# Modulation rows made by GpSimd inside the attention, in paced pieces, with loads from its own queue

## The chip, the core and the metric

One core of a Trainium2 chip runs the whole layer in one launch. The engines are TensorE (PE), VectorE (DVE), ScalarE (ACT), GpSimd (POOL) and SyncE (SP), each with its own instruction stream that it runs in order; they meet by semaphores. The metric is the device time in microseconds (us).

## The reference, cut to what matters

One layer of a diffusion backbone: 1024 latent tokens and 256 context tokens, width 1024, fp32. The part that the change touches:

```python
mod = jnp.einsum('bd,de->be', jax.nn.silu(c), w_mod[layer]) + b_mod[layer]
sh1, sc1, g1, sh2, sc2, g2 = jnp.split(mod[:, None, :], N_MOD, axis=-1)
hx = modulate(rmsnorm(x, norm1_g[layer]), sh1, sc1)          # h * (1 + scale) + shift
q_x, k_x, v_x, u_x, b_x, c_x, ga_x, gc_x = split_projection(hx @ w_in[layer])
o_attn = latent_window_attention(q, k, v, k_ctx, v_ctx, attn_sink[layer])
y_conv = short_conv_mixer(u_x, b_x, c_x, conv_w[layer])      # B * conv3(C * u)
x = x + g1 * gated_merge(o_attn, y_conv, ga_x, gc_x, w_proj_attn, w_proj_conv, w_out)
hx2 = modulate(rmsnorm(x, norm2_g[layer]), sh2, sc2)
x = x + g2 * expert_choice_moe(hx2, ...)
```

The modulation rows g1, sh2, sc2 and g2 (parts 2 to 5 of mod, 1024 values each) are each a product of one vector, silu(c), with a 1024x1024 piece of w_mod. They are first read behind the products stage below.

## The kernel before

The program runs five stages, one behind the other: the modulation for the first norm, the norm and the projections of q, k and v (to 252 us); the attention (252 to 582); the products stage (611 to 1085); output projection, second norm and router; the experts (from 1234). Products in fp32 are made from a high and a low part of each operand: three matmuls each.

**Attention.** A unit is one of 4 key groups and one of 8 blocks of 128 queries: 32 units, numbered n. In the loop over units (L690 on) the step s of unit n first transposes the softmax rows p of one block of keys (`turn`, L630; ACT L633 and DVE L634 split the result), then makes the scores of one head of unit n+2 (`scores`, L605/606; DVE L608; exponential on ACT L613); behind the fourth head GpSimd scales that unit's four p tiles (`normalise`, L625). Then `pour(1)` takes one step of the gate projection (three matmuls, L40/42/44), a filler for TensorE, and `values` makes two matmuls (L642/643). The order of the engines' instructions is set by the scheduler from this code, each engine's stream being fixed when the program is built. At units 4, 10, 16 and 22 `x_sums` is emitted: ten additions or subtractions of 128x512 on GpSimd (L657), splits on ACT and DVE, and writes.

**Products stage.** 20 pairs of column blocks, each multiplied by Strassen's scheme in Winograd's form: seven block products (slots 0 to 6) of 12 matmuls of 128x512 (L795), 84 per pair. Here the order of all engines is written out by hand (`in_order`); `at_turn(n, slot, f)` puts work at a slot of pair n. VectorE makes each pair's weight sums (L829/830, L839/840), splits (L810) and results (L1107, L1140, `quad` L867 to L889; L875 is the addition q<-q or q<-psT,q). Pairs 2, 5, 8 and 11 add the convolution: ACT L907, then four steps on VectorE (L908, L910), both operands in SBUF. Beside it:

- `Row` (four rows): each load of 128x1024 from w_mod goes out on SP's queue (L740), ScalarE scales it by silu(c) (L743), GpSimd adds it to the sum (L745); then a split (ACT L751, POOL L752), and `total` at slot 6 of pairs 2, 5, 8 and 12: four matmuls with a column of ones (L760), two additions of the bias on VectorE (L761), a write to rowd (L766).
- `sums_of` on GpSimd (L930): four subtractions of 128x512 for each block of the convolution's output (pairs 4, 7, 10, 13) and four for each of four blocks of the attention's output (`o_rows`, turns 17, 38, 59 and 68, in pairs 2, 5, 8 and 9).
- From pair 11 on, the operands of the next products are split by ACT (L973) and VectorE and GpSimd (L974), and two multiplications move to GpSimd (L881, L980).

Of the kernel before, what the change touches and what calls it, by code (L numbers as in the profile page):

```python
# [27 lines left out]
def hybrid_layer(ctx, tc, x, c, cx, c_ctx, w_mod, b_mod, norm1_g, w_in, attn_sink, conv_w,  # L28
# [702 lines left out]

    class Row:


        def __init__(self, n, part):
            self.n, self.part, self.w = n, part, {}

        def load(self, k):
            self.w[k] = mp_slot(4 + k % 2 if k else 6)
            nc.sync.dma_start(out=self.w[k], in_=w_mod[k * 128:(k + 1) * 128, self.part * 1024:self.part * 1024 + 1024])  # L740

        def add(self, k):
            nc.scalar.activation(out=self.w[k], in_=self.w[k], func=AF.Copy, scale=sf[:, 0, k:k + 1])  # L743
            if k:
                nc.gpsimd.tensor_tensor(out=self.acc, in0=self.w[k], in1=self.acc, op=OP.add)  # L745
            else:
                self.acc = self.w[k]

        def split(self):
            self.halves = [mp.tile([128, 1024], FR, name=f"mp{4 + i}") for i in range(2)]  # L750
            nc.scalar.copy(out=self.halves[0], in_=self.acc)  # L751
            nc.gpsimd.tensor_tensor(out=self.halves[1], in0=self.acc, in1=self.halves[0].bitcast(F32), op=OP.subtract)  # L752
            self.row = self.acc[0:1]
            nc.gpsimd.dma_start(out=self.row, in_=b_mod[:, self.part * 1024:self.part * 1024 + 1024])

        def total(self, pf):
            br = self.row
            for hf in range(2):
                for i in range(2):
                    nc.tensor.matmul(pf[hf][0:1], lhsT=onesr, rhs=self.halves[i][:, hf * 512:hf * 512 + 512], start=(i == 0), stop=(i == 1))  # L760
# [1093 lines left out]
```

## Time and profile before

| what | us |
|---|---|
| median of 3 runs (1834.47 to 1837.97) | 1836.47 |
| the profiled run | 1830.33 |
| its span | 1828.5 |
| busy in the span: PE / DVE / ACT / POOL | 1716.5 / 1459.1 / 1040.5 / 557.4 |
| attention, 330.0 us: PE / POOL busy | 327.0 / 138.8 |
| pairs 0 to 10, 261.6 us (611 to 872.6): PE / DVE / POOL busy | 228.1 / 206.1 / 129.1 |
| output projection to router, 148.7 us: PE busy | 121.4 |
| experts, 594.0 us: PE / DVE busy, DMA share | 580.8 / 559.7, 0.93 |

The table is read by stage: a span has one engine that limits it in one stage and another in the next. Durations are those of one profiled execution, so a sum is made against 1830.33 and then set beside the median. The granted clock of TensorE is a share of its higher level, 2.4 GHz; 0.50 is the lower level, 1.2 GHz.

### The profile page before, as it was taken

What the parts mean: (1) busy time and instruction counts of PE and PEld (TensorE: products, weight loads), DVE (VectorE), ACT (ScalarE), POOL (GpSimd) and SP (SyncE); (2) the same over time, 40 slices, a digit from 0 to 9 for tenths busy, and PEclk for the clock granted to TensorE, in tenths of its full rate; (3) what the DMA queues carried; (4) which work ended last, traced back from release to release, by engine and by line L of the source; (5) the groups of instructions that cost most, each with busy time, mean ns of one, the idle gap of its engine ahead of it and who ended that gap; (6) DMA issues with size and microseconds to landing.
All of it is one profiled execution on the core that took longest, in us unless ns stands there. A gap on an engine that the chain in (4) does not pass through costs nothing.

```text
span 1828.5 us, 24343 instructions
## 1 busy us (share of the span) xinstructions
PE 1716.5 (94%) x8421; PEld 1384.8 (76%) x8421; DVE 1459.1 (80%) x1996; ACT 1040.5 (57%) x1482; POOL 557.4 (30%) x366
## 2 busy tenths in 40 slices
PE   8999999999999989878798898959999999999997
PEld 5778888888888867666567677847888888888875
DVE  6756568778775488897887876578999999999997
ACT  6642267767774334333445343226777877877875
POOL 0001226255231245365763301241024223223101
PEclk8999999999999999998899999979999999999999
DMA  9353354344413737437657245778999999999955
GB/s 343 129 162 115 127 189 142 94 138 126 148 55 121 255 107 220 133 121 230 230 160 252 72 151 190 257 280 323 341 398 396 387 393 399 384 397 398 340 196 196
DMA packets 210861, 415.71 MB, mean 227 GB/s; under 512 B 17643, under 2 KB 107051, under 8 KB 209202
## 3 DMA queue, kind: packets, MB, share of 16 engines
q1 hardware_dynamic: 182226, 368.20, 56.3%
q0 software_dynamic: 6912, 25.51, 4.7%
q10 hardware_dynamic: 21600, 20.45, 3.2%
q8 instruction: 66, 1.08, 0.2%
q14 instruction: 57, 0.47, 0.1%
HBM read 343.31 MB, written 70.80 MB: 226 GB/s over the span
## 4 chain that ended last, share of the span: by engine, by line
PE 63%; DVE 14%; issue 4%; ACT 2%; DMA 2%; POOL 1%; SPq 0%; ACTq 0%; POOLq 0%; DVEq 0%
PE psA L1659 19%; PE psB L1659 5%; PE psF L1659 5%; PE w L795 5%; PE psT L630 3%; PE psT L795 3%; PE psA L1225 3%; PE psF L40 2%; PE psF L42 2%; PE psF L44 2%; PE psB L643 2%; PE psB L642 2%; PE psA L605 2%; PE psA L606 2%; DVE x L810 2%
## 5 line engine op out<-in xcount | busy, mean ns | idle before, releaser
L1659 PE MATMUL psA<-part,xeh 128*128 128x512 f32 x1024 | 281.9, 392 | 0.5 <-ACT xeh L1647 0.5
L1659 PEld LDWEIGHTS psA<-part,xeh 128*128 128x128 f32 x1024 | 191.3, 188 | 39.9 <-ACT xeh L1647 1.0
L1694 POOL DMA_INDIRECT md<-ye,idxs x15 | 107.9, 7190 | 213.3 <-DVE ye L1691 213.3
L1659 PE MATMUL psA<-part,xel 128*128 128x512 f32 x512 | 163.4, 390 | 0.0
L625 POOL TENSOR_SCALAR p<-p,l 128x640 f32<-128x640 f32 (+1 forms) x128 | 99.6, 797 | 176.5 <-DVE l L623 51.3
L1517 DVE TENSOR_TENSOR part<-er,part 128x1024 fp32r<-128x1024 f32 x118 | 138.4, 1219 | 5.3 <-ACT part L1515 2.0
L1515 ACT CAST part<-er 128x1024 fp32r<-128x1024 f32 x118 | 123.7, 1056 | 32.9 <-PE psA L1659 19.9
L809 ACT CAST whi<-raw 128x1024 fp32r<-128x1024 f32 x40 | 42.0, 1049 | 173.7 <-DVE raw L840 110.0
L634 DVE TENSOR_TENSOR tl<-psT,th 128x512 fp32r<-128x512 f32 x152 | 103.9, 687 | 26.5 <-ACT th L633 25.1
L608 DVE CUSTOM_DVE_ANT_0 sn<-psA,msk,nsink 128x640 f32<-128x640 f32 (+1 forms) x128 | 107.3, 843 | 21.7 <-PE psA L606 21.1
L745 POOL TENSOR_TENSOR mp<-mp,mp 128x1024 f32<-128x1024 f32 x28 | 73.3, 2618 | 152.5 <-ACT mp L743 151.7
L633 ACT CAST th<-psT 128x512 fp32r<-128x512 f32 x152 | 88.3, 584 | 50.4 <-PE psT L630 49.5
L613 ACT ACTIVATE p<-sn,nm 128x640 f32<-128x640 f32 (+1 forms) x128 | 103.0, 806 | 19.5 <-DVE nm L608 17.6
L1659 PEld LDWEIGHTS psA<-part,xel 128*128 128x128 f32 x512 | 96.3, 188 | 20.5 <-DVE xel L1648 0.3
L1517 DVE TENSOR_TENSOR part<-mh,part 128x1024 fp32r<-128x1024 f32 x88 | 105.0, 1219 | 5.4 <-ACT part L1515 2.4
L1517 DVE TENSOR_TENSOR part<-ml,part 128x1024 fp32r<-128x1024 f32 x88 | 105.3, 1219 | 4.4 <-ACT part L1515 1.6
L1515 ACT CAST part<-ml 128x1024 fp32r<-128x1024 f32 x88 | 92.2, 1052 | 26.3 <-PE psA L1659 17.6
L1515 ACT CAST part<-mh 128x1024 fp32r<-128x1024 f32 x88 | 92.1, 1052 | 25.2 <-PE psA L1659 16.5
L1517 DVE TENSOR_TENSOR part<-mp,part 128x1024 fp32r<-128x1024 f32 x85 | 100.8, 1220 | 6.6 <-ACT part L1515 3.8
L1515 ACT CAST part<-mp 128x1024 fp32r<-128x1024 f32 x88 | 91.9, 1052 | 24.5 <-PE psA L1659 16.1
L1659 PE MATMUL psB<-part,hhh 128*128 128x512 f32 x256 | 98.6, 396 | 0.2 <-ACT hhh L1647 0.2
L810 DVE TENSOR_TENSOR wlo<-raw,whi 128x1024 fp32r<-128x1024 f32 x40 | 52.9, 1322 | 55.4 <-ACT whi L809 55.4
(501 smaller groups left out, 4695.4 us busy)
## 6 DMA issues: line engine op xcount, KB each, us to landing
raw<-in_w_in_dram SPq DMA_DIRECT2D x49, 512.0 KB, 5.2
er<-in_w_exp_down_dram SPq DMA_DIRECT2D x47, 512.0 KB, 8.7
er<-in_w_exp_up_dram SPq DMA_DIRECT2D x38, 512.0 KB, 6.0
mp<-in_w_exp_gate_dram SPq DMA_DIRECT2D x36, 512.0 KB, 6.3
mh<-in_w_exp_up_dram SPq DMA_DIRECT2D x33, 512.0 KB, 5.6
ml<-in_w_exp_up_dram SPq DMA_DIRECT2D x33, 512.0 KB, 6.5
mp<-in_w_mod_dram SPq DMA_DIRECT2D x32, 512.0 KB, 4.9
er<-in_w_exp_gate_dram SPq DMA_DIRECT2D x32, 512.0 KB, 5.8
```

The costliest lines, as they stand in the source:

```text
L608: nc.vector.tensor_tensor_reduce(out=sn, in0=sp[:, 512 - n:768], in1=msk.rearrange("p a b -> p (a b)")[:, mo * 128:mo * 128 + n + L], op0= ...
L613: nc.scalar.activation(out=p, in_=sn, func=AF.Exp, scale=-1.0, bias=self.nm4[:, h:h + 1], accum_out=self.l4[:, h:h + 1])
L625: nc.gpsimd.tensor_scalar(self.pr[h], self.pr[h], l4[:, h:h + 1], 1.0, op0=OP.mult, op1=OP.mult)
L633: nc.scalar.copy(out=th, in_=pt)
L634: nc.vector.tensor_tensor(out=tl, in0=pt, in1=th.bitcast(F32), op=OP.subtract)
L745: nc.gpsimd.tensor_tensor(out=self.acc, in0=self.w[k], in1=self.acc, op=OP.add)
L795: nc.tensor.matmul(ps_, lhsT=w[a][:, o + k], rhs=xs[b][:, k], start=(first and k + a + b == 0), stop=(k == 3 and a == 1), skip_group_check ...
L810: tt(out=lo, in0=src, in1=hi.bitcast(F32), op=OP.subtract)
L1515: nc.scalar.copy(out=hi, in_=raw)
L1517: eng.tensor_tensor(out=lo, in0=raw, in1=hi.bitcast(F32), op=OP.subtract)
L1659: nc.tensor.matmul(outs[s], lhsT=lh[:, k], rhs=wt[:, s * 512:s * 512 + 512], start=(k == 0 and n == 0), stop=(k == NK - 1 and n == 2))
L1694: nc.gpsimd.indirect_dma_start(out=md, out_offset=bass.IndirectOffsetOnAxis(ap=idxs[:, e:e + 1], axis=0), in_=ye, in_offset=None, compute_ ...
```

## The change

The class `Row` goes. A generator, `mod_row(n)`, makes a row on GpSimd alone: it loads 128x1024 of w_mod from GpSimd's own queue, scales it (L716), adds it to the sum (L718), issues the next load, and hands back; then bias loads; then two matmuls with columns of `onehot` (L730) put the two halves of the sum of all partitions on two rows, VectorE adds the bias (L731), and SP writes rowd. The loaded tile "o2" has one buffer, and so has the sum "o1". `x_sums` hands back three times in between, and `o_sums` makes the subtractions for two of the attention's four blocks. `pool_work` chains four rows, four x_sums and two o_sums; the attention's loop takes one piece at s = 1 and one at s = 4 of every unit, so a row is 10 pieces, five units. In the products stage the subtractions for the convolution's output and for the two other blocks go to VectorE, and the two quads of the last pair move behind the first matmuls of the output projection and the router's row.

```diff
+    onehot = consts.tile([128, 4], F32, name="onehot")
...
+        for i in range(3):
+            nc.vector.tensor_scalar(onehot[:, i:i + 1], ones, float(i == 1), None, op0=OP.mult)
...
+    os_cm = tc.tile_pool(name="os", bufs=1)
+    osp = os_cm.__enter__()
+
+    def mod_row(n):
+        part = n + 2
+        acc = osp.tile([128, 1024], F32, name="o1")
+
+        def load(k):
+            w = osp.tile([128, 1024], F32, name="o2")
+            nc.gpsimd.dma_start(out=w, in_=w_mod[k * 128:(k + 1) * 128, part * 1024:part * 1024 + 1024])
+            return w
+
+        w = load(0)
+        yield
+        for k in range(NK):
+            nc.gpsimd.tensor_scalar(w if k else acc, w, sf[:, 0, k:k + 1], 1.0, op0=OP.mult, op1=OP.mult)
+            if k:
+                nc.gpsimd.tensor_tensor(out=acc, in0=w, in1=acc, op=OP.add)
+            if k < NK - 1:
+                w = load(k + 1)
+                yield
+        small = osp.tile([128, 1024], F32, name="o2")
+        br, nr = small[0:2, 0:512], small[0:2, 512:1024]
+        nc.gpsimd.dma_start(out=br, in_=b_mod[:, part * 1024:part * 1024 + 1024].rearrange("o (h f) -> (o h) f", h=2))
+        if part == 4:
+            nc.gpsimd.dma_start(out=nr, in_=norm2_g.rearrange("o (h f) -> (o h) f", h=2))
+        yield
+        pf = psT()[0:2]
+        for hf in range(2):
+            nc.tensor.matmul(pf, lhsT=onehot[:, 1 - hf:3 - hf], rhs=acc[:, hf * 512:hf * 512 + 512], start=(hf == 0), stop=(hf == 1))
+        nc.vector.tensor_tensor(out=br, in0=pf, in1=br, op=OP.add)
+        if part == 4:
+            nc.vector.scalar_tensor_tensor(out=br, in0=br, scalar=1.0, in1=nr, op0=OP.add, op1=OP.mult)
+        nc.sync.dma_start(out=rowd[n].rearrange("(h f) -> h f", h=2), in_=br)
+        yield
+
+    def pool_work():
+        for n in range(4):
+            yield from mod_row(n)
+        for ks in range(4):
+            yield from x_sums(ks)
+        for ks in range(2):
+            yield from o_sums(ks)
+
+    def o_sums(ks):
+        o1, o2 = (osp.tile([128, 2, 512], F32, name=f"o{a}") for a in (1, 2))
+        o = o_rows(ks, o1.rearrange("p a b -> p (a b)"), [o2[:, 0], o2[:, 1]])
+        yield
+        sums_of(nc.gpsimd, *o)
+        sums_out(*o)
+        yield
+
+    pool_left = pool_work()
...
-        if n in (4, 10, 16, 22):
-            x_sums((n - 4) // 6)
...
             pour(1)
+            if s in (1, 4):
+                next(pool_left, None)
             if s > 0:
                 cur.values(s - 1)
+    for _ in pool_left:
+        pass
     at_cm.__exit__(None, None, None)
+    os_cm.__exit__(None, None, None)
...
-    class Row:
...
     for m in range(4):
-        at_turn(3 * m + 4, 2, lambda: sums_of(*st["ys"]))
+        at_turn(3 * m + 4, 2, lambda: sums_of(nc.vector, *st["ys"]))
         at_turn(3 * m + 4, 5, lambda: sums_out(*st["ys"]))
 
-    def row_start(r):
-        st["row"] = Row(r, r + 2)
-
-    for r in range(4):
-        at_turn(3 * r, 0, lambda r=r: row_start(r))
-        for k, (a, b) in enumerate(((0, 2), (1, 3), (2, 4), (5, 7), (6, 8), (9, 11), (10, 12), (13, 15))):
-            at_turn(3 * r, a, lambda k=k: st["row"].load(k))
-            at_turn(3 * r, b, lambda k=k: st["row"].add(k))
-        at_turn(*((3 * r + 2, 2) if r < 3 else (11, 6)), lambda: st["row"].split())
-
-    for ks, b in enumerate((17, 38, 59, 68)):
-        at_turn(0, b - 5, lambda ks=ks: o_rows(ks))
-        at_turn(0, b, lambda: sums_of(*st["o"]))
+    for ks, b in ((2, 17), (3, 38)):
+        at_turn(0, b - 5, lambda ks=ks: o_late(ks))
+        at_turn(0, b, lambda: sums_of(nc.vector, *st["o"]))
         at_turn(0, b + 3, lambda: sums_out(*st["o"]))
     at_turn(12, 5, late_mults)
...
-            if n in (2, 5, 8, 12) and slot == 6:
-                st["row"].total([psT(), psT()] if n % 2 == 0 else [psa.tile([128, 512], F32, name=f"w{c}") for c in range(2)])
             cur.product(slot)
...
         out_weight(j)
-    for q in (0, 2):
-        prev.quad(q)
     wide.close()
...
     out_proj(0, range(0, 6), pas[0])
     bc = router_row()
+    for q in (0, 2):
+        prev.quad(q)
     out_proj(1, range(0, 4), pas[1])
```

How the instructions stand on three engines follows. In the names, p are the softmax rows, l their factors, o the new tiles o1 and o2, mp, gs and raw are buffers of the products stage.

GpSimd (POOL) in the attention, before, units 7 to 10: the normalisations alone.

```order
L625 TENSOR_SCALAR p<-p,l_2933 128x512 x4
L625 TENSOR_SCALAR p<-p,l_3069 128x512 x4
L625 TENSOR_SCALAR p<-p,l_3207 128x640 x4
L625 TENSOR_SCALAR p<-p,l_3321 128x640 x4
L625 TENSOR_SCALAR p<-p,l_3439 128x640 x4
L625 TENSOR_SCALAR p<-p,l_3577 128x640 x4
```

GpSimd with the change, units 9 to 11, at the end of row 1:

```order
L628 TENSOR_SCALAR p<-p,l_3243 128x640 x4
L716 TENSOR_SCALAR o_3354<-o_3354,sf 128x1024
L718 TENSOR_TENSOR o_2999<-o_3354,o_2999 128x1024
L710 DMA o_3414<-in_w_mod_dram 128x1024
L716 TENSOR_SCALAR o_3414<-o_3414,sf 128x1024
L718 TENSOR_TENSOR o_2999<-o_3414,o_2999 128x1024
L710 DMA o_3480<-in_w_mod_dram 128x1024
L628 TENSOR_SCALAR p<-p,l_3365 128x640 x4
L716 TENSOR_SCALAR o_3480<-o_3480,sf 128x1024
L718 TENSOR_TENSOR o_2999<-o_3480,o_2999 128x1024
L724 DMA o_3537<-in_b_mod_dram 2x512
L628 TENSOR_SCALAR p<-p,l_3491 128x640 x4
```

Two steps of the row stand between two units' normalisations, each load directly behind the addition before it.

TensorE (PE) in the attention, before, from the last step of unit 4 to the first transposes of unit 5 (x are halves of the hidden state, th and tl the split transposes):

```order
L630 MATMUL psT<-identr,p 128x128 x4
L40 MATMUL psF<-x_696,whi 128x512
L42 MATMUL psF<-x_697,whi 128x512
L44 MATMUL psF<-x_696,wlo 128x512
L642 MATMUL psB<-th,v2t 128x512
L643 MATMUL psB<-tl,v2t 128x512
L40 MATMUL psF<-x_752,whi 128x512
L42 MATMUL psF<-x_753,whi 128x512
L44 MATMUL psF<-x_752,wlo 128x512
L642 MATMUL psB<-th,v2t 128x512
L643 MATMUL psB<-tl,v2t 128x512
L630 MATMUL psT<-identr,p 128x128 x4
```

With the change, the same place:

```order
L40 MATMUL psF<-x_697,whi 128x512
L42 MATMUL psF<-x_698,whi 128x512
L44 MATMUL psF<-x_697,wlo 128x512
L730 MATMUL psT<-o_2310,onehot 2x512 x2
L645 MATMUL psB<-th,v2t 128x512
L646 MATMUL psB<-tl,v2t 128x512
L40 MATMUL psF<-x_753,whi 128x512
L42 MATMUL psF<-x_754,whi 128x512
L44 MATMUL psF<-x_753,wlo 128x512
L645 MATMUL psB<-th,v2t 128x512
L646 MATMUL psB<-tl,v2t 128x512
L633 MATMUL psT<-identr,p 128x128 x4
```

The two matmuls of row 0 stand seven products ahead of the first transposes of unit 5; those of rows 1 to 3 stand so ahead of units 10, 15 and 20.

VectorE (DVE) in pair 2, before:

```order
L810 TENSOR_TENSOR wlo<-raw,whi 128x1024
L908 SCALAR_TENSOR_TENSOR mp_6990<-mp_6781,cols,mp_6990 128x1023
L910 SCALAR_TENSOR_TENSOR mp_6990<-mp_6781,cols,mp_6990 128x1023
L908 SCALAR_TENSOR_TENSOR mp_6991<-mp_6782,cols,mp_6991 128x1023
L910 SCALAR_TENSOR_TENSOR mp_6991<-mp_6782,cols,mp_6991 128x1023
L810 TENSOR_TENSOR x_7014<-raw,x_7014 128x512
L1140 TENSOR_TENSOR q<-w_6903,q 128x512
L761 TENSOR_TENSOR mp_6647<-psT,mp_6647 1x512 x2
L839 TENSOR_TENSOR raw<-raw 128x512
L840 TENSOR_TENSOR raw<-raw 128x512
```

With the change:

```order
L851 TENSOR_TENSOR wlo<-raw,whi 128x1024
L949 SCALAR_TENSOR_TENSOR mp_7144<-mp_6956,cols,mp_7144 128x1023
L951 SCALAR_TENSOR_TENSOR mp_7144<-mp_6956,cols,mp_7144 128x1023
L688 TENSOR_TENSOR mp_7038<-mp_7038 128x512
L688 TENSOR_TENSOR mp_7038<-gs,mp_7038 128x512
L688 TENSOR_TENSOR gs<-gs,mp_7038 128x512
L688 TENSOR_TENSOR gs<-gs 128x512
L949 SCALAR_TENSOR_TENSOR mp_7145<-mp_6957,cols,mp_7145 128x1023
L951 SCALAR_TENSOR_TENSOR mp_7145<-mp_6957,cols,mp_7145 128x1023
L851 TENSOR_TENSOR x_7168<-raw,x_7168 128x512
L1154 TENSOR_TENSOR q<-w_7064,q 128x512
L880 TENSOR_TENSOR raw<-raw 128x512
```

Four subtractions came in between the two halves of the convolution, and the row's two additions left.

## Rows read from the trace of the kernel before

**Rows 1.** Busy time by stretch: us, PE, PEld, DVE, ACT, POOL, clock, DMA share, GB/s

```profile
252.00:582.00 330.00, 327.01 (x1894) 277.52 (x1894) 256.58 (x537) 236.15 (x498) 138.79 (x158) 1.00 0.37 110
...
611.00:872.60 261.60, 228.10 (x941) 180.21 (x940) 206.14 (x182) 95.40 (x110) 129.14 (x60) 0.95 0.51 164
...
640.00:660.00 20.00, 20.00 (x88) 16.20 (x87) 14.94 (x13) 7.29 (x8) 8.02 (x4) 1.00 0.53 167
```

**Rows 2.** Timeline (start, duration): first matmuls of pairs 0 and 11, two first copies

```profile
611.16 0.63 PE L795 MATMUL w<-t,whi 128*128 128x512 f32 x2
614.15 0.58 ACT L1095 COPY q<-w 128x512 f32<-128x512 f32 x1 [1.98 <-PE w L795]
633.48 0.59 ACT L1095 COPY q<-psT 128x512 f32<-128x512 f32 x1 [0.55 <-PE psT L795]
871.90 0.63 PE L795 MATMUL psT<-t,whi 128*128 128x512 f32 x2
```

**Rows 3.** Waits of TensorE, 660 to 1120 us: waiter, releaser, us, times, longest

```profile
PE psT L795 <- DVE mp L761: 13.8, 2, 6.9
PE w L795 <- DVE mp L761: 6.9, 1, 6.9
PE psT L1333 <- DVE bc L1325: 1.8, 1, 1.8
```

**Rows 4.** Timeline in pair 2: VectorE, GpSimd, and TensorE behind its wait

```profile
667.06 2.57 DVE L908 SCALAR_TENSOR_TENSOR mp<-mp,cols,mp 128x1023 f32<-128x1023 f32 x1 [0.78 <-ACT mp L907]
670.86 2.14 POOL L930 TENSOR_TENSOR mp<-gs,mp 128x512 f32<-128x512 f32 x1
679.20 1.22 PE L795 MATMUL psT<-t,whi 128*128 128x512 f32 x2 [6.92 <-DVE mp L761]
683.21 0.64 PE L795 MATMUL psT<-t,whi 128*128 128x512 f32 x2
```

**Rows 5.** Durations of single lines, ns: least, median, most; from and to

```profile
L875 DVE TENSOR_TENSOR q<-q x15: 678/684/2880, 660.1 to 1073.5; 128x512 f32<-128x512 f32 x15
L875 DVE TENSOR_TENSOR q<-psT,q x12: 673/680/684, 756.1 to 1051.5; 128x512 f32<-128x512 f32 x12
L908 DVE SCALAR_TENSOR_TENSOR mp<-mp,cols,mp x8: 1271/2404/5581, 667.1 to 889.7; 128x1023 f32<-128x1023 f32 x8
L625 POOL TENSOR_SCALAR p<-p,l x128: 690/799/1775, 252.0 to 567.3; 128x640 f32<-128x640 f32 x96, 128x512 f32<-128x512 f32 x32
L1249 POOL TENSOR_TENSOR raw<-raw,whi x7: 2343/2392/2408, 1125.0 to 1200.8; 128x1024 f32<-128x1024 f32 x7
L774 PE MATMUL psT<-g2r,ones x4: 587/587/692, 1293.0 to 1294.4; 1*128 1x512 f32 x4
```

**Rows 6.** Timeline of GpSimd: the first normalisation, and an issue behind an operation

```profile
251.97 2.71 POOL L625 TENSOR_SCALAR p<-p,l 128x512 f32<-128x512 f32 x4 [13.60 <-DVE l L623]
1203.46 0.58 POOL L1250 DMA_DIRECT2D hd<-raw  x1 [0.30 <-POOL raw L1249]
```

**Rows 7.** Timeline of TensorE: the first transposes of units 5, 10, 15, 20

```profile
296.75 0.60 PE L630 MATMUL psT<-identr,p 128*128 128x128 f32 x4
348.05 0.49 PE L630 MATMUL psT<-identr,p 128*128 128x128 f32 x3
406.70 0.60 PE L630 MATMUL psT<-identr,p 128*128 128x128 f32 x4
461.09 0.60 PE L630 MATMUL psT<-identr,p 128*128 128x128 f32 x4
```

**Rows 8.** DMA issues of the whole run: queue, count, size, median us to landing

```profile
raw<-in_w_out_dram SPq DMA_DIRECT2D x6, 512.0 KB, 3.8
mp<-in_b_mod_dram POOLq DMA_DIRECT2D x4, 4.0 KB, 1.8
msk<-in_masks_dram POOLq DMA_DIRECT2D x1, 576.0 KB, 5.3
```

**Rows 9.** Line L1250, writes of 512 KB on GpSimd's queue

```profile
DMA to landing us min/median/max: 3.0/5.8/8.1
```

More of the change, by code (lines that the diff above doesn't have):

```diff
@@ L677, in x_sums, with sums_of, sums_out @@
                 nc.sync.dma_start(out=xd[n * 2:n * 2 + 2, hl, :, ks].rearrange("n p f -> p n f"), in_=v.bitcast(F32))
+    def sums_of(eng, which, ks, p11, p12, p21, p22):
+        for o_, a, b in ((p11, p12, p11), (p12, p22, p12), (p22, p22, p11), (p21, p21, p22)):
+            eng.tensor_tensor(out=o_, in0=a, in1=b, op=OP.subtract)
+    def sums_out(which, ks, p11, p12, p21, p22):
+        for n, p in enumerate((p11, p12, p22, p21)):
+            nc.sync.dma_start(out=sums[which][n, ks], in_=p)
@@ new lines, in o_rows @@
+    def o_rows(ks, p1, p2):
+        nc.sync.dma_start(out=p1, in_=od[ks * 128:(ks + 1) * 128])
+        for th in range(2):
+            nc.sync.dma_start(out=p2[th], in_=od[512 + ks * 128:512 + (ks + 1) * 128, th * 512:th * 512 + 512])
+        return 0, ks, p1[:, 0:512], p1[:, 512:1024], *p2
+    os_cm = tc.tile_pool(name="os", bufs=1)
[29 more added lines that the diff above has]
+        nc.sync.dma_start(out=rowd[n].rearrange("(h f) -> h f", h=2), in_=br)
+        yield
@@ L730, in hybrid_layer @@
     psa = new_wide()
-    class Row:
[L735 to L760, printed above, removed]
-                nc.vector.tensor_tensor(out=br[:, hf * 512:hf * 512 + 512], in0=pf[hf][0:1], in1=br[:, hf * 512:hf * 512 + 512], op=OP.add)
-            if self.part == 4:
-                nr = mp_slot(4)[0:1]
-                nc.sync.dma_start(out=nr, in_=norm2_g)
-                nc.vector.scalar_tensor_tensor(out=br, in0=br, scalar=1.0, in1=nr, op0=OP.add, op1=OP.mult)
-            nc.sync.dma_start(out=rowd[self.n:self.n + 1], in_=br)
     def spread_row(dst, src):
@@ L803, in hybrid_layer @@
     NP = len(cols3)
-    onesr = tmpp.tile([128, 2], FR, name="onesr")[:, 0:1]
-    nc.vector.tensor_copy(out=onesr, in_=ones)
     k0, k1 = slice(0, 4), slice(4, 8)
@@ L925, in signal, with o_late @@
             nc.scalar.activation(out=self.sig[q], in_=self.sig[q], func=AF.Sigmoid)
-    def sums_of(which, ks, p11, p12, p21, p22):
-        for o_, a, b in ((p11, p12, p11), (p12, p22, p12), (p22, p22, p11), (p21, p21, p22)):
-            nc.gpsimd.tensor_tensor(out=o_, in0=a, in1=b, op=OP.subtract)
-    def sums_out(which, ks, p11, p12, p21, p22):
-        for n, p in enumerate((p11, p12, p22, p21)):
-            nc.sync.dma_start(out=sums[which][n, ks], in_=p)
-    def o_rows(ks):
-        p1 = mp_slot(7)
-        nc.sync.dma_start(out=p1, in_=od[ks * 128:(ks + 1) * 128])
-        p2 = [stage.tile([128, 512], F32, name="gs", bufs=2) for th in range(2)]
-        for th in range(2):
-            nc.sync.dma_start(out=p2[th], in_=od[512 + ks * 128:512 + (ks + 1) * 128, th * 512:th * 512 + 512])
-        st["o"] = (0, ks, p1[:, h0], p1[:, h1], *p2)
+    def o_late(ks):
+        st["o"] = o_rows(ks, mp_slot(7), [stage.tile([128, 512], F32, name="gs", bufs=2) for th in range(2)])
     takes = (("t1", (tx, "t1")), ("t3", (tx, "t3")), ("b11", (0, 0)), ("b22", (1, 1)), ("t4", (tx, "t4")), ("t2", (tx, "t2")), ("b21", (1, 0)))
```

3 lines of the change are left out of this document (2 added, 1 removed).

## The prediction

> **What bounds the kernel now.** I read the table of stages first, since one share of busy time for 1828 us mixes stages with different limits. In the attention (252 to 582 us) TensorE is busy 327.0 of 330.0 us at full clock, while GpSimd is busy 138.8: what TensorE is made to wait for there is lost, one for one [rows 1]. The products stage behind it is not bound so. Its 20 pairs of 84 matmuls should take 19.33 us each, the distance of two undisturbed pairs' first copies (633.48 - 614.15), but the eleven pairs 0 to 10 take 871.90 - 611.16 = 260.74 us [rows 2], and 11 x 19.33 = 212.6. So 48.1 us are lost in eleven pairs.
>
> Next I read who ends the waits there. Three times TensorE waits 6.9 us for VectorE's sum of a modulation row, 20.7 us together [rows 3]; VectorE itself is late by then. In pair 2 one of its four convolution steps takes 2.57 us, and a subtraction of GpSimd beside them 2.14 [rows 4]; over the run that step takes from 1.27 to 5.58 us. The addition q<-q, both operands in SBUF, takes 0.678 to 2.88, and the same with one operand in PSUM never over 0.684 [rows 5]. So VectorE is stretched where both of its operands and those of GpSimd lie in SBUF. A gap also costs afterwards: behind the first 6.9 us TensorE stood at its lower level (0.50 granted, 1.2 GHz), with nine matmuls from 679.20 to 683.21 [rows 4], 4.0 us where 88 matmuls in 20 us [rows 1] give 2.0. Two us more per gap.
>
> **Products stage: what goes.** Out of it go 28 row additions, 4 row splits and 32 subtractions on GpSimd, the rows' 32 loads on SP's queue, 36 operations on ScalarE (not late itself), 16 matmuls and 9 one-row operations on VectorE with the three waits. In come 24 subtractions of 128x512 on VectorE. GpSimd has nothing left in pairs 0 to 9, so VectorE's work should return to its shortest durations: 14.94 us in an undisturbed 20-us slice [rows 1], plus four convolution steps of 1.27 in every third pair (5.1), plus four subtractions of 0.68 (2.7) in the two pairs where a part of the attention's output is summed too. That is 22.7 us against TensorE's 19.33, in pairs 2 and 5 alone; the next pair has 4.4 us to spare, but its second product needs a split early in it. I leave 1 us of wait each in pairs 3 and 6, and 0.5 for the rest: 48.1 - 2.5 = 45.6. In pairs 11 to 19 GpSimd keeps the operand splits and late multiplications; only the last row goes, and I take 3 us. The broadcast row's 1.8 us wait [rows 3] goes too: the two last quads now stand behind the matmuls that it feeds, which hide them; if that cover is missing, their six VectorE operations of 0.68 cost 4. Gain: 45.6 + 3 + 1.8 = 50.4, with ends 25 (VectorE stays late) and 57.
>
> **Attention: what comes.** The forty pieces spread a row over five units. But a load, its scaling and its addition share one buffer: GpSimd issues load k+1 behind addition k, and scaling k+1 waits for its landing. So a step takes L + scaling + addition, L being issue to landing. Scaling: 0.690 us at 512 columns and 0.799 at 640 [rows 5], so 0.690 + 4 x 0.109 = 1.13 at 1024 (estimate). Addition: 2.39 at this shape in a quiet stretch [rows 5]. Gaps: 0.30 before an issue that follows an operation [rows 6], 0.08 between operations (estimate). A step is L + 3.9. The four normalisations of a unit (3.1 us at 128x640: 4 x 0.799) stand mostly behind a load, and are hidden by it.
>
> TensorE's two matmuls that sum the row stand, by the order, seven products ahead of the first transposes of units 5, 10, 15 and 20 (296.75, 348.05, 406.70, 461.09 [rows 7]), 1.6 us before them. TensorE runs its instructions in order: it waits for the row, and everything of the attention behind it waits too.
>
> Row 0: two loads are out before normalisation 0, which ends at 251.97 + 2.71 = 254.7 [rows 6]. Addition 1 ends 3.6 later, six steps remain: 258.3 + 6 (L + 3.9).
>
> L is what the trace doesn't show for this queue and shape. Bounds: 512 KB went out on GpSimd's queue in 3.0 at least, 5.8 in the median and 8.1 at most [rows 9] (writes, several at once); 576 KB of masks came in by it in 5.3, and 512 KB of output weights on SP's queue in 3.8 [rows 8]. The last is nearest (same shape and direction, moderate traffic: the attention's DMA share is 0.37 [rows 1]); I add 0.3 since GpSimd's issue alone took 0.58 [rows 6], and take L = 4.1, with 3.0 and 5.8 as ends. So row 0 is ready at 306.3 instead of 295.1: a wait of 11.2.
>
> Row 1 starts only when TensorE has summed row 0, VectorE has added the bias and the row is written out: 2 x 0.59 for matmuls (the nearest fp32 row with 512 columns [rows 5]), 0.7, 1.8 for the write, as for the bias's 4 KB [rows 8], 0.5 of gaps: 4.2 (estimate). Then L + 1.13, seven steps, and a normalisation between scaling and addition (2.7): 35.3 + 8L = 68.1, against 51.3 between the units: 16.8. Row 2: two normalisations outside loads (5.9), two more subtractions of the x sums (2.6), and two groups of four subtractions that outlast their load by 1.4 each: 76.7 against 58.65: 18.0. Row 3: 0.7 more of handoff: 33.3 + 8L = 66.1 against 54.39: 11.7. The intervals are GpSimd's, so TensorE's slow clock after each gap is absorbed in the next wait; only behind the last it counts, 2.0, with its own matmuls, 1.2. Sum: 11.2 + 16.8 + 18.0 + 11.7 + 3.2 = 60.9. Per us of L it is 28, less below 3.8, since about 13 of the loads stand over a normalisation that takes as long.
>
> First comes the row's fact: 512 KB on GpSimd's queue needed 3.0 us at least [rows 9]. The Trainium skill, "DMA: Bandwidth & Descriptors", section "Anatomy of one DMA — SWDGE (gpsimd) path", gives about 2.0 us fixed plus bytes over 436 GB/s, 3.2 us here by the page (estimate); the 5.3 and the median 5.8 lie well over it, the minimum a little under. By it the sum would be that of the first rival, 1829.5.
>
> **The sum.** 60.9 - 50.4 = 10.5 us slower. Against the profiled run's own 1830.33 (span 1828.5 and 1.8 around it) that is 1840.8; the median of the runs shown, 1836.47, is 6.1 higher, so 1847 and, with the matmuls of the sums at the lower clock (up to 1.2 more each), 1848. The attention pays what the products stage gets, because it has no slack on TensorE, and a single buffer leaves GpSimd idle during each load.
>
> **Rivals.** First, the other side: the loads land in 3.0 to 3.5 us. At 3.2 the 15 loads without cover save 13.5 and the 13 others 3.9: 43.5 against 50.4, 7 us faster, 1829.5; it decides at L of about 3.6, where the price of the attention falls to that of the gain. For it: the minimum of 3.0, one load at a time, DMA share 0.37. Against it: 3.8 for the quickest such weight read in the median, on a queue with shorter issues. Second, slow landings: at 5.3 as for the masks, 60.9 + 28 x 1.2 = 94.5, so 1836.5 + 44 = 1881; from 5.0 to 5.8, 1872 to 1895. The reads of keys, values and queries and the writes of the outputs run beside. Third, the relief doesn't come: VectorE gets 24 subtractions, stays late behind the convolutions, and only half of the 50 is found: 1836.5 + 60.9 - 25 = 1872.
>
> **How the numbers follow.** Forecast case (L 3.6 to 5, relief as reckoned) 0.47, of it 0.36 slower by over 0.2%, 0.08 within, 0.03 faster; 0.2%, 3.7 us, is about what a measurement of this kernel can tell from no change. Loads at 3.0 to 3.6: 0.27, of it 0.22 faster, 0.05 same. Slow loads 0.15, no relief 0.08, both slower. A remaining 0.03, faster: TensorE's matmuls are not reached as early as the order says. Faster 0.28, same 0.13, slower 0.59. The range from 1815 (L at 3.0 and a gain of 57, with some room: 1836.5 + 40 - 57 = 1820) to 1888 leaves out some 0.15.
>
> **What would show it.** In the changed profile: four waits of TensorE of 10 to 18 us ahead of the row's two matmuls, released by GpSimd's last addition, with the clock at 0.50 behind; issue to landing of the row loads near 4.1; the transposes of unit 20 some 58 us later. Behind it, eleven pairs in about 215 us, q<-q back at 0.68 and the convolution steps at 1.27, waits of about a us in pairs 3 and 6. The forecast is wrong in the attention if the four waits are under 5 us each, and in the products stage if the eleven pairs still take over 225 us.

## The result, and the profile after

The changed kernel takes 1888.85 us (median of 4 runs, 1887.09 to 1891.95) against 1835.82 before: a ratio of 1.029 with the interval 1.0272 to 1.0307, 53 us slower. The forecast was 1848, slower, with a range that ends at 1888, just below. The profiled run of the changed kernel is 1891.95, its span 1890.2.

Busy time of the changed kernel by stretch, columns as in [rows 1]: first the attention up to unit 20, then its rest, then pairs 0 to 10 and pairs 11 to 19 of the products stage.

```profile
252.00:547.00 295.00, 231.66 (x1216) 182.97 (x1216) 186.76 (x354) 149.84 (x322) 206.03 (x195) 0.88 0.39 117
547.00:684.00 137.00, 122.08 (x678) 100.99 (x677) 99.71 (x188) 86.19 (x175) 82.49 (x76) 0.95 0.48 153
...
716.80:931.50 214.70, 214.43 (x925) 173.31 (x924) 149.85 (x195) 60.77 (x77) 0.00 (x0) 1.00 0.32 104
931.50:1138.00 206.50, 186.99 (x754) 146.61 (x753) 170.67 (x165) 88.59 (x107) 74.56 (x33) 0.94 0.52 174
```

In the attention TensorE now stands idle for 63 us ahead of unit 20 and at a granted clock of 0.88; in pairs 0 to 10 it is busy for 214.43 of 214.70. The marks that place the difference are transposes and a pair's first copy. Counted by the kernel (a unit transposes 4 or 5 blocks of keys), the marks of [rows 7] at 461.09 and of the two first rows here are not the units' first transposes: they are the second block of unit 20 and the third of unit 31. The first of unit 20 stand at 459.37 before and 545.12 after, those of unit 31 at 575.45 and 681.08; by these marks the first two differences below are 85.8 and 19.9, so the table holds.

```profile
546.96 0.60 PE L633 MATMUL psT<-identr,p 128*128 128x128 f32 x4
...
683.81 0.60 PE L633 MATMUL psT<-identr,p 128*128 128x128 f32 x4
...
719.84 0.59 ACT L1109 COPY q<-w 128x512 f32<-128x512 f32 x1 [2.03 <-PE w L838]
...
934.51 0.59 ACT L1109 COPY q<-psT 128x512 f32<-128x512 f32 x1 [1.39 <-PE psT L838]
```

| stretch | before, us | after, us | difference |
|---|---|---|---|
| to the second transposes of unit 20 [rows 7] | 461.09 | 546.96 | +85.9 |
| from there to the third of unit 31 | 117.1 | 136.9 | +19.8 |
| from there to pair 0's first copy [rows 2] | 36.0 | 36.0 | 0 |
| pairs 0 to 10, copy to copy | 261.3 | 214.7 | -46.6 |
| pairs 11 to 18, copy to copy | 193.6 | 188.0 | -5.6 |

So 105.7 us were lost in the attention and 52.2 won in the products stage: 53.5, against 53.0 between the medians. Behind pair 18 the two profiled executions differ by 8 us more, 759.5 and 767.7. That stretch lies between 759 and 764 us in the four profiled kernels that have the old products stage and between 762 and 768 in the ten that have the new one, so most of the 8 us is spread between executions; some 3 may be the change's. One place in it is seen: the wait of 1.8 us for the router's row [rows 3] is gone, as forecast, but TensorE's wait for the next rows of the hidden state has grown in its place (before, then after):

```profile
PE psT L1269 <- DVE raw L1235: 2.3, 2, 1.8
...
PE psT L1281 <- DVE raw L1247: 6.6, 2, 4.8
```

All ten kernels with the two quads moved have 6.4 to 6.8 us there, the four without 2.3 to 4.0; that the moved quads cause it is likely and was not tested.

The gain of the products stage is about what the forecast said. A convolution step of VectorE has one duration now, where [rows 5] had 1271 to 5581:

```profile
L949 DVE SCALAR_TENSOR_TENSOR mp<-mp,cols,mp x8: 1276/1277/1278, 767.4 to 945.6; 128x1023 f32<-128x1023 f32 x8
```

The loss in the attention is larger than forecast, and has two places. TensorE's waits from 240 to 690 us, chosen rows (waiter, releaser, us, times, longest):

```profile
PE psT L730 <- POOL o L718: 47.4, 4, 15.1
PE psB L645 <- ACT th L636: 12.1, 3, 9.6
PE psT L633 <- POOL p L628: 11.3, 9, 4.7
PE psB L646 <- DVE tl L637: 5.7, 5, 2.5
```

**The rows.** The end of row 0 on GpSimd's and TensorE's timelines, the landing times of the row loads, and GpSimd's wait for them:

```profile
302.36 0.61 POOL L710 DMA_DIRECT2D o<-in_w_mod_dram  x1 [0.30 <-POOL o L718]
306.55 1.11 POOL L716 TENSOR_SCALAR o<-o,sf 128x1024 f32<-128x1024 f32 x1 [3.58 <-DMA o<-in_w_mod_dram]
307.74 2.34 POOL L718 TENSOR_TENSOR o<-o,o 128x1024 f32<-128x1024 f32 x1
310.13 3.41 PE L730 MATMUL psT<-o,onehot 128*2 128x512 f32 x4 [10.53 <-POOL o L718]
...
DMA to landing us min/median/max: 3.8/4.5/9.4
...
POOL o L716 <- DMA o<-in_w_mod_dram: 76.5, 28, 8.9
```

Load, scaling and addition follow each other, as the order said. A load takes 4.5 us, not 4.1, and the two sum matmuls 3.41 (3.57 in the other rows), not 1.2; the granted clock just ahead of the first sum is 0.50:

```profile
305.00:310.00 5.00, 0.00 (x0) 0.00 (x0) 0.00 (x0) 0.00 (x0) 3.37 (x2) 0.50 0.10 40
```

The three other rows end in waits of 8.82, 15.15 and 12.92 us, each followed by the same sum:

```profile
383.54 3.57 PE L730 MATMUL psT<-o,onehot 128*2 128x512 f32 x4 [8.82 <-POOL o L718]
465.72 3.57 PE L730 MATMUL psT<-o,onehot 128*2 128x512 f32 x4 [15.15 <-POOL o L718]
539.74 3.57 PE L730 MATMUL psT<-o,onehot 128*2 128x512 f32 x4 [12.92 <-POOL o L718]
```

**Behind the rows.** Here the forecast had set nothing. Three engines around 610 us:

```profile
610.07 3.02 SPq L692 DMA_DIRECT2D sums<-o  x3
613.85 0.57 SPq L683 DMA_DIRECT2D xd<-whi  x1
617.32 1.05 ACT L680 CAST whi<-raw 128x1024 fp32r<-128x1024 f32 x1 [10.82 <-DMA xd<-whi]
619.92 2.13 DVE L681 TENSOR_TENSOR wlo<-raw,whi 128x1024 fp32r<-128x1024 f32 x1 [10.04 <-DMA xd<-wlo]
620.52 0.79 PE L645 MATMUL psB<-th,v2t 128*128 128x512 f32 x1 [9.63 <-ACT th L636]
...
SPq L692 <- POOL o L688: 18.8, 6, 11.9
```

Read from the end: TensorE waits 9.63 us for a split of the softmax rows on ScalarE; ScalarE has stood 10.82 us in front of a split of the x sums, whose buffer is free only when an earlier write has left; that write stands on SP's queue behind the writes of the attention's sums, which wait 11.9 us for GpSimd's subtractions; and these come behind the x sums on GpSimd. The change has packed the x sums into units 20 to 25: 30 of their 40 operations run from 540 to 623 us, ten already in row 2.

### The profile page after: what moved, and what is told of

Read it like the earlier page. It is cut to its first block, busy times and chain, and to the rows that moved or that the text cites. A ratio compares the mean times of both kernels' runs of the same rounds, so it can differ in the third digit from the quotient of the medians.

```text
span 1890.2 us, 24223 instructions
## 1 busy us (share of the span) xinstructions
PE 1737.0 (92%) x8421; PEld 1390.9 (74%) x8421; DVE 1427.8 (76%) x2018; ACT 1004.9 (53%) x1446; POOL 545.4 (29%) x403
## 4 chain that ended last, share of the span: by engine, by line
PE 72%; DVE 8%; DMA 7%; POOL 7%; issue 4%; ACT 2%; SPq 0%; POOLq 0%; ACTq 0%; DVEq 0%
PE psA L1673 19%; PE w L838 7%; PE psT L838 5%; PE psB L1673 5%; PE psF L1673 5%; DMA o<-in_w_mod_dram 4%; PE psA L1237 3%; POOL o L718 3%; PE psA L400 2%; PE psA L398 2%; PE psA L399 2%; PE psF L838 2%; PE psT L633 2%; PE psF L40 2%; PE psF L42 1%
## 5 line engine op out<-in xcount | busy, mean ns | idle before, releaser
L1529 ACT CAST part<-er 128x1024 fp32r<-128x1024 f32 x118 | 123.7, 1056 | 32.9 <-PE psA L1673 19.9
L611 DVE CUSTOM_DVE_ANT_0 sn<-psA,msk,nsink 128x640 f32<-128x640 f32 (+1 forms) x128 | 107.4, 843 | 24.7 <-PE psA L609 16.6
L922 POOL TENSOR_TENSOR mp<-q,mp 128x512 f32<-128x512 f32 x15 | 24.4, 1652 | 293.8 <-DVE q L916 280.2
L633 PE MATMUL psT<-identr,p 128*128 128x128 f32 x608 | 96.4, 277 | 11.5 <-POOL p L628 11.3
L1529 ACT CAST part<-mp 128x1024 fp32r<-128x1024 f32 x88 | 92.0, 1053 | 26.6 <-PE psA L1673 16.6
L633 PEld LDWEIGHTS psT<-identr,p 128*128 128x128 f32 x608 | 77.3, 143 | 35.5 <-POOL p L628 15.4
```

Source lines behind the costliest of these rows:

```text
L611: nc.vector.tensor_tensor_reduce(out=sn, in0=sp[:, 512 - n:768], in1=msk.rearrange("p a b -> p (a b)")[:, mo * 128:mo * 128 + n + L], op0= ...
L633: nc.tensor.transpose(pt[:, h * 128:(h + 1) * 128], self.pr[h][:, ci * 128:(ci + 1) * 128], ident)
L1529: nc.scalar.copy(out=hi, in_=raw)
```

## Experiments

Times are medians; "before" of each group ran on the same chip. Delays are read from the span's start, and the attention starts at 252.6 to 258.6 us in the profiled kernels (252.7 before), so a delay can hold up to 6 us that come from ahead of it. Three questions: what made the rows so dear, what happened behind them, and what gave the 52 us.

### Two buffers, and two loads only

The load moved ahead of the scaling, with a second buffer:

```diff
-            w = osp.tile([128, 1024], F32, name="o2")
+            w = osp.tile([128, 1024], F32, name="o2", bufs=2)
...
         for k in range(NK):
+            nxt_w = load(k + 1) if k < NK - 1 else None
...
-                w = load(k + 1)
+                w = nxt_w
```

> The changed kernel with two buffers for the loaded tile, load k+1 issued ahead of scaling k (room for it: the query tiles have 3 buffers instead of 4, one copy 1 instead of 2). Serial-load theory: the four rows delay the first transposes of unit 20 by 85.9 us because a landing of 4.5 us stands in each of 28 steps; with the landing behind the operations a step is issue, scaling, addition and gaps (4.5 us) plus the unit's normalisation (3.1 us per unit), so GpSimd itself needs about 58 us per row against 51 to 59 of TensorE: the delay falls to 25 to 40, the time to about 1838 (1828 to 1850). Rival, GpSimd's queue is the limit (two loads at once land in 8 us): the delay stays above 60, the time above 1865.

1849.94 us against 1834.23 (ratio 1.0084, 1.0062 to 1.0106): 16 us slower than its own before, so 37 us of the 53 are back, and the time is at the upper end of the range expected. The second transposes of unit 20 come at 513.82, a delay of 52.7 (4.9 of it a later start of the attention), not the 25 to 40 expected, but below the rival's 60. At the row sums no wait of note is left. What is left is GpSimd's stream itself, which TensorE meets at the softmax rows:

```profile
POOL p L628 <- DVE l L626: 39.5, 9, 10.3
POOL o L717 <- DMA o<-in_w_mod_dram: 23.0, 7, 10.0
...
PE psT L633 <- POOL p L628: 12.4, 12, 6.0
PE psB L645 <- ACT th L636: 11.7, 4, 9.6
PE psB L646 <- DVE tl L637: 8.0, 8, 2.2
PE psB L645 <- DVE oo L652: 6.5, 3, 4.7
```

Seven waits for landings remain, 23.0 us, with the normalisations behind them. The 9.6 us in front of L645 is the jam behind the rows, again.

Loads left out:

```diff
-            if k < NK - 1:
+            if k == 0:
                 w = load(k + 1)
+            if k < NK - 1:
                 yield
```

> The changed kernel with loads 0 and 1 of each row alone; scalings and additions all stay, working on the second tile again and again, so the rows' values are not those of the reference. Serial-load theory: 24 landings of 4.5 us leave the chain, but about half of them covered a normalisation, which stands on it now; a row needs some 56 to 62 us, with the x sums in row 2 some 70: the delay of unit 20 falls from 85.9 to 25 to 40, time 1835 to 1850. Rival, the delay comes from GpSimd's operations and the sums on TensorE, not the landings: delay above 60, time above 1865.

1847.53 us against 1834.23 (ratio 1.0081, 1.0057 to 1.0105); the second transposes of unit 20 come at 504.91, a delay of 43.8, a little over the 25 to 40 expected. So with 24 of 32 landings gone the price of the rows falls by half: 42 of 85.9 us were landings that nothing covered, and 44 are GpSimd's 3.5 us of operations per step together with the normalisations, which then stand on the chain, and the sums. Both this and the two buffers stand well under the rival's 1865.

### Without rows

```diff
-        w = load(0)
-        yield
         for k in range(NK):
-            nc.gpsimd.tensor_scalar(w if k else acc, w, sf[:, 0, k:k + 1], 1.0, op0=OP.mult, op1=OP.mult)
-            if k:
-                nc.gpsimd.tensor_tensor(out=acc, in0=w, in1=acc, op=OP.add)
-            if k < NK - 1:
-                w = load(k + 1)
-                yield
+            yield
...
-        nc.vector.tensor_tensor(out=br, in0=pf, in1=br, op=OP.add)
```

> The changed kernel without the rows' loads, scalings, additions and matmuls; a row is its bias alone, so this part of the computation is left out. The pieces keep their places. Theory: the 85.9 us up to unit 20 go, the 19.8 behind it stay, the gain of 52 in the products stage stays: 1889 - 86 = 1803 (1799 to 1808). Rival, the loss behind unit 20 was a late effect of the rows (a block's load waits for the buffer of row 3): it goes too, 1783 to 1790.

1800.18 us against 1834.23, as the theory said. Unit 20 (its second transposes) comes at 458.80, 2.3 earlier than before the change, and the stretch from there to unit 31 (its third transposes, as in the table) takes 134.9 against 117.1: the jam behind the rows stays. The rival is out: the loss behind unit 20 is not an echo of the rows. Its long wait is the same one:

```profile
PE psB L645 <- ACT th L636: 9.4, 1, 9.4
```

### The attention's sums out of the attention

```diff
-        for ks in range(2):
-            yield from o_sums(ks)
...
-    for ks, b in ((2, 17), (3, 38)):
+    for ks, b in ((2, 17), (3, 38), (0, 59), (1, 68)):
```

> The changed kernel, but the subtractions for all four blocks of the attention's output on VectorE in the products stage (pairs 2, 5, 8, 9); none in the attention. Theory: the 19.8 us lost behind unit 20 come from SP's queue, where the writes of these sums stand ahead of the writes of the x sums whose buffers ScalarE and VectorE wait for; they go, and at most 2 us come back in pairs 8 to 10: about 1871 (1867 to 1875). Rival, the x sums are simply too dense in units 20 to 25 (two buffers for their splits): only 0 to 6 us go, 1883 to 1889.

1872.27 us (16.6 less than the change), as the theory said. From unit 20 to unit 31 it takes 123.2: 13.7 of the 19.8 are gone with these sums (their loads, subtractions and writes left together, so the writes alone are not shown), and 6.1 stay with the dense x sums. The long wait for ScalarE's split is gone, and the rows' waits are nearly what they were:

```profile
PE psT L730 <- POOL o L718: 43.7, 4, 14.0
PE psT L633 <- POOL p L628: 10.1, 9, 4.6
PE psB L646 <- DVE tl L637: 4.3, 5, 1.5
PE psB L645 <- ACT th L636: 2.7, 4, 1.4
```

### The relief by itself

The last two edits together, and the x sums back at units 4, 10, 16 and 22:

> The changed kernel without the rows' loads, scalings, additions and matmuls (a row is its bias alone, that part of the computation is left out), with the x sums at units 4, 10, 16 and 22 and all sums of the attention's output on VectorE in the products stage: the relief of the products stage by itself. Theory: 1836 - 52 = 1784 (1780 to 1789), the attention as long as before the change. Rival, part of the loss in the attention comes from something else (pool of tiles, order of the writes): 1792 or more.

1786.81 us against 1835.69 (ratio 0.9735, 0.9712 to 0.9758): 48.9 us, and from the first transposes of unit 0 to the third of unit 31 the attention takes 325.5 us, as before the change. This is the gain of the change, without its price.

### Which part of the products stage gave it

The 24 subtractions back on GpSimd, rows still in the attention:

```diff
-        at_turn(3 * m + 4, 2, lambda: sums_of(nc.vector, *st["ys"]))
+        at_turn(3 * m + 4, 2, lambda: sums_of(nc.gpsimd, *st["ys"]))
...
-        at_turn(0, b, lambda: sums_of(nc.vector, *st["o"]))
+        at_turn(0, b, lambda: sums_of(nc.gpsimd, *st["o"]))
```

> The changed kernel with the 24 subtractions of the products stage back on GpSimd; the rows stay in the attention. It tells which part of the move out of the products stage gave the 52 us. Theory, VectorE is stretched wherever GpSimd works beside it on SBUF operands, in proportion to GpSimd's time: before, rows and splits were 83 us of it, sums about 52; now about 35 us of sums alone stay, so 5 to 18 of the 52 us are lost again: 1894 to 1907. Rival, the sums cost VectorE more than they would GpSimd (23 us of work in a convolution pair against 19.4 of TensorE): 2 to 5 us faster, 1884 to 1887.

1890.34 us against 1835.69, the same as the change. Pairs 0 to 10 take 213.7 us, 0.9 less than with the sums on VectorE. Neither expectation holds: with the rows gone, the sums cost nothing on GpSimd. The reason that the trace shows is their time. Nothing stands ahead of them on GpSimd, so those set for pair 2 run at 744 to 751 us, while TensorE is still at pair 1, as soon as their loads land, and the convolution of pair 2 starts at 768:

```profile
744.43 1.29 POOL L688 TENSOR_TENSOR mp<-mp 128x512 f32<-128x512 f32 x1 [70.32 <-DMA mp<-od]
...
L949 DVE SCALAR_TENSOR_TENSOR mp<-mp,cols,mp x8: 1276/1278/1280, 767.9 to 945.1; 128x1023 f32<-128x1023 f32 x8
```

In the kernel before, without the rows' additions and split subtractions on GpSimd:

```diff
-            if k:
-                nc.gpsimd.tensor_tensor(out=self.acc, in0=self.w[k], in1=self.acc, op=OP.add)
-            else:
+            if k == 0:
                 self.acc = self.w[k]
...
-            nc.gpsimd.tensor_tensor(out=self.halves[1], in0=self.acc, in1=self.halves[0].bitcast(F32), op=OP.subtract)
+            nc.scalar.copy(out=self.halves[1], in_=self.acc)
```

> The kernel before without GpSimd's 28 row additions and 4 split subtractions (rows keep one eighth of their sum, the rest is left out); loads, scalings, ScalarE's copies, matmuls and one-row additions stay, and so do GpSimd's 32 sums. Theory of the prediction: pairs 0 to 10 return to about 19.4 us, 38 to 50 us won: 1785 to 1797. Rival, the loads on SP's queue, ScalarE's scalings or the one-row sums carry it: less than 25 won, above 1810.

1805.36 us against 1836.85 (ratio 0.9831, 0.9806 to 0.9855): 31.5 won, between theory and rival. Pairs 0 to 10 take 235.3 us, 26.0 less than before. The three pairs with a convolution still take 26 us each, and the rows of one show what is left there: GpSimd's bias load waits for ScalarE's split, the sums behind it start with the convolution, and each engine makes the other late.

```profile
666.44 0.56 POOL L752 DMA_DIRECT2D mp<-in_b_mod_dram  x1 [94.86 <-ACT mp L750]
666.95 2.48 DVE L906 SCALAR_TENSOR_TENSOR mp<-mp,cols,mp 128x1023 f32<-128x1023 f32 x1 [1.72 <-ACT mp L905]
667.02 1.31 POOL L928 TENSOR_TENSOR mp<-mp 128x512 f32<-128x512 f32 x1
668.41 2.17 POOL L928 TENSOR_TENSOR mp<-gs,mp 128x512 f32<-128x512 f32 x1
669.46 2.20 DVE L908 SCALAR_TENSOR_TENSOR mp<-mp,cols,mp 128x1023 f32<-128x1023 f32 x1
```

And without the rows' last step, the three waits that [rows 3] show:

```diff
-            for hf in range(2):
-                for i in range(2):
-                    nc.tensor.matmul(pf[hf][0:1], lhsT=onesr, rhs=self.halves[i][:, hf * 512:hf * 512 + 512], start=(i == 0), stop=(i == 1))
-                nc.vector.tensor_tensor(out=br[:, hf * 512:hf * 512 + 512], in0=pf[hf][0:1], in1=br[:, hf * 512:hf * 512 + 512], op=OP.add)
```

> The kernel before without the rows' last step: no matmuls with the column of ones, no one-row additions (a row is its bias alone; that part is left out), while loads, scalings, additions on GpSimd and splits stay in the products stage. Theory of the prediction, VectorE is late because it is stretched beside GpSimd: the three waits of 6.9 us move to the next product that needs VectorE, at most 15 of the 48 us are won: 1820 to 1834. Rival, the rows cost by the place of these one-row sums in the order of TensorE and VectorE: 30 us or more are won, under 1806.

1831.51 us against 1836.85: 5 us, as the theory said. The 20.7 us of waits at the one-row additions are not their cost; the wait goes to the next product that needs VectorE's or ScalarE's splits. The two longest waits of TensorE in pairs 0 to 10 are now:

```profile
PE psF L791 <- ACT x L805: 11.6, 2, 6.4
PE w L791 <- ACT x L805: 7.5, 2, 5.2
```

### A slower pace, and three versions

If five units were just too few for a row, a row over seven to eight units would do, with one buffer still:

```diff
-            if s in (1, 4):
+            if s == 1 or s == 4 and n % 2:
```

(with one more piece ahead of the sums, the x sums at their old units, and all of the attention's sums late on VectorE.)

> As e6_spread in pace and places, but with the one buffer, the load behind the addition and the scaling on GpSimd as in the change. A row's chain is 74 us, seven units are about 75. Theory, the deadline of five units was the fault and not the buffer as such: waits for the rows under 5 us each, 1798 to 1810. Rival, the chain is behind at each sum anyway, since the x sums and the normalisations stand in it too: 8 to 15 us each, 1820 to 1845.

1862.27 us against 1835.69: slower than both expected. No wait at the row sums is left, so the deadline is not what remains. GpSimd waits 73.8 us in 25 places for landings, and now the normalisations behind these waits are late:

```profile
POOL o L716 <- DMA o<-in_w_mod_dram: 73.8, 25, 9.8
...
PE psT L633 <- POOL p L628: 32.6, 35, 7.2
```

With two buffers in that pace, and the scaling on ScalarE:

```diff
-            nc.gpsimd.tensor_scalar(w if k else acc, w, sf[:, 0, k:k + 1], 1.0, op0=OP.mult, op1=OP.mult)
+            nc.scalar.activation(out=w if k else acc, in_=w, func=AF.Copy, scale=sf[:, 0, k:k + 1])
```

> A version made from the causes: two buffers and the load ahead, scaling on ScalarE, a row spread over 7 to 8 units with a piece of slack before its matmuls (they stand at units 7, 14, 21 and 29), the x sums at units 4, 10, 16 and 22 as before the change, all sums of the attention's output on VectorE in the products stage. If waits and the jam on SP's queue were the whole loss, the attention takes 330 us as before plus four sums of 1.7 to 3.4, and the products stage keeps its gain: 1836 - 50 + 10 = 1796 (1788 to 1804). Rival, GpSimd as a whole is too full for the normalisations: TensorE waits for them 10 to 30 us, 1806 to 1826.

1828.86 us against 1835.69 (ratio 0.9964, 0.995 to 0.9977), 60 less than the change and 7 less than the kernel before: the best complete version here, and faster than the kernel before, by little. That is outside the theory's range and just above the rival's, and the rival's sign did not come either: TensorE no longer waits for softmax rows. ScalarE has taken the waits over: 18.7 us in front of 14 scalings, and its splits, which TensorE needs, stand behind.

```profile
ACT o L717 <- DMA o<-in_w_mod_dram: 18.7, 14, 4.8
...
PE psB L646 <- DVE tl L637: 12.5, 11, 3.4
PE psB L645 <- ACT th L636: 10.4, 10, 4.2
```

A third buffer, with loads three steps ahead (two other tiles gave up room):

> As e6_spread, with three buffers for the loaded tile and each load issued three steps ahead (room: query tiles 2 buffers, two copies 1 each). In e6 ScalarE waits 18.7 us in 14 places for a landing in front of its scaling, and the exponentials and splits that TensorE needs stand behind it. Theory: these waits fall under 5 us, the attention gets 15 to 30 us shorter, 1800 to 1815. Rival, ScalarE and GpSimd are simply too full, or the missing buffers cost as much: 1822 or more.

1833.69 us against 1836.85: the rival. ScalarE still waits 18.3 us for landings, in 10 places: buffers alone do not bring the loads ahead of their use. A likely reason is that GpSimd issues them from its own stream, where it now waits 10.6 us for ScalarE's scalings ahead of three of the loads. How much of the rest is ScalarE's and GpSimd's load as such is left open.

From the other side, rows kept in the products stage, clear of the convolution:

```diff
-((0, 2), (1, 3), (2, 4), (5, 7), (6, 8), (9, 11), (10, 12), (13, 15))
+((0, 2), (1, 3), (2, 4), (4, 6), (5, 7), (7, 9), (8, 10), (10, 12))
-        at_turn(*((3 * r + 2, 2) if r < 3 else (11, 6)), lambda: st["row"].split())
+        at_turn(3 * r + 1, 6, lambda: st["row"].split())
-            if n in (2, 5, 8, 12) and slot == 6:
+            if n in (2, 5, 8, 11) and slot == 3:
```

(and all sums on VectorE.)

> A version from the other side: the kernel before, rows kept in the products stage on SP, ScalarE and GpSimd, but a row's loads and additions packed into the two pairs without convolution (last addition at turn 12 of its three pairs instead of 15, split at the second pair's last slot), its one-row sums at slot 3 instead of 6 of pairs 2, 5, 8 and 11 and so ahead of the convolution on VectorE, and all sums on VectorE. Nothing new in the attention. Theory: what cost 46 us was GpSimd's work lying beside VectorE's convolution steps; with it out of their way the steps take 1.28 us, pairs 0 to 10 come to 19.4 to 21, the attention stays as before: 1792 to 1803. Rival, the additions stretch VectorE in the other pairs just as much, so that they are late there (slack of 4.4 us): 1815 or more.

1834.12 us against 1834.41: nothing. The convolution steps are at 1.27 in the median, but pairs 1 to 10 take 22 to 27 us each, with a convolution or without: the additions stretch VectorE's splits instead (1.23 us alone), and ScalarE waits 23.0 us for the tighter loads (13.1 before).

```profile
654.96 2.66 DVE L810 TENSOR_TENSOR wlo<-raw,whi 128x1024 fp32r<-128x1024 f32 x1 [2.30 <-ACT whi L809]
658.60 2.55 DVE L810 TENSOR_TENSOR x<-raw,x 128x1024 fp32r<-128x1024 f32 x1 [0.99 <-ACT x L809]
...
ACT mp L743 <- DMA mp<-in_w_mod_dram: 23.0, 7, 4.7
```

So moving GpSimd's additions away from the convolution wins nothing here: they meet others of VectorE's operations, and ScalarE is later. TensorE waits about as long for ScalarE's splits (14.4 us) as for VectorE's (12.3); the two causes are not separated.

## Why the prediction was right and where it was wrong

**The products stage: right.** 48.1 us lost in eleven pairs, 45.6 to come back, 46.6 came; in the pairs behind them 3 were set and 5.6 came. The last 1.8, for the router's row, were not won: that wait went, and another grew by more. The whole gain was 50.4 by the sum and 48.9 by the kernel that has the relief alone. The waits of a microsecond set for pairs 3 and 6 did not come: a copy is 1.8 us late there, and TensorE is busy all the same (214.43 of 214.70). The reason holds with one correction: the rows' work gave the relief, 26 us by its own additions; once it was gone, moving the sums to VectorE gave nothing. The other 20 us fit sums that the rows' splits held back until they met the convolution, but the rows' loads, scalings, splits and one-row sums left with them, and no run takes these apart. The stretch follows the form that the prediction read from [rows 5]. The Trainium skill, "SBUF — State Buffer", section "SBUF: two separate sides", says that a VectorE operation with two SBUF inputs and a GpSimd operation that reads SBUF exclude each other for a whole instruction; the split of 2.66 us beside GpSimd's additions, 1.23 alone, agrees.

**The waits for the rows: right in place and kind, too small in size.** Up to unit 20 the sum gave 57.7 in four waits and 3.2 behind the last; 85.9 came. The waits themselves are 47.4 in all, one of them under 10: since the intervals are GpSimd's, the longer sums, matmuls at the lower clock and 11.3 us of waits for softmax rows take their part of them. Between the ends of the four rows on GpSimd the terms can be checked one by one: from row 0's last addition (310.08) to row 1's (383.48) 73.4 us, where 35.3 + 8 x 4.1 = 68.1 stood. Eight loads at 4.5 instead of 4.1 are 3.2, the sum 3.5 instead of 1.2 is 2.3: 5.5, which closes it. Over the four rows the load's 0.4 makes 11 us (30 loads on the chain) and the sum matmuls 7 (three times; behind the last one 3.6 stood against 3.2). Another 1.7 lie in the marks of [rows 7]: the first transposes of units 10, 15 and 20 stand at 347.50, 404.97 and 459.37, so the intervals to set against GpSimd's are shorter by that. Of the remaining 5, a normalisation in row 3 that outlasts its load is 2.1. The load was mis-sized within its stated ends, though the row taken as nearest was a read on another queue; GpSimd's own 3.0 was a write's and no load came under 3.8. The sum was mis-sized by its row: 0.59 is a matmul with one partition of input, and not behind a wait. Here each of the two matmuls is recorded as two, and TensorE has just idled for 10 us: the clock granted in the 5 us ahead of it is 0.50, and 3.41 us are the time of eight times 512 columns at 1.2 GHz. That the clock could add 1.2 per sum was said, but on the wrong base. The Trainium skill, "FP8 and Floating Point Precision", section "TensorE Precision Notes", gives four passes for true fp32, which is what these eight for two matmuls are.

**The step that failed.** It is the price of the attention, 60.9 us by the sum and 105.7 by the trace, and in it first the stretch behind unit 20, which the sum put at nothing without a reason. For the x sums nothing was set beyond two groups in row 2, for the attention's sums nothing at all. They cost 19.8 us: 13.7 go when the attention's sums leave, 6.1 stay with the dense x sums, and without any row 17.8 are still there. The longest wait of it, 9.6 us, comes through SP's queue, on which the writes of the attention's sums were queued ahead of others; it is gone in the run without these sums. The prediction asked who waits behind GpSimd, and did not ask it of the queue that GpSimd's results leave by. The second part is of size: the landing, 4.5 for 4.1 (11 us), and the sum matmuls, 3.5 for 1.2 (7 us). That the normalisations mostly hide behind a load held, but for the 2.1 us in row 3. With both places at their measured size the account closes: 85.9 + 19.8 - 52.2 = 53.5.

**The rivals.** Short landings (3.0 to 3.5, and the 3.2 of the estimate) did not come, nor landings of 5 and more in the median; 4.5 lies within the forecast case. The measured 1888.85 lies among the 1872 to 1895 of the second rival, but not for its reason. The third did not come either: the relief was there. What took the time past the forecast was another cause, a jam on a queue, and it was not among the rivals.

## What to carry to other kernels

Work moved into a stage that has no slack on its limiting engine is paid for there, even on an idle engine, if its results or its waits stand in front of something that the limiting engine needs: a wait for a landing in an in-order stream holds all that follows, and when a second buffer came and the wait moved from GpSimd to ScalarE, 33 us were won and ScalarE was late instead. Follow each moved operation to the queue by which its result leaves, and look what is queued behind it. Of a step that runs load, use, load, use in one buffer, the landing belongs to the sum each time; pricing it needs a row of the same queue, direction and shape.
